# Weight pieces of half the columns, and a final norm whose last block is halved and whose one half ACT scales

## The chip, the cores and the metric

The kernel runs on one core of one Trainium2 chip. A core has five engines with instruction queues of their own: TensorE (PE, matmuls; its weight loads are listed apart as PEld), VectorE (DVE), ScalarE (ACT), GpSimd (POOL) and SyncE (SP, which here only starts DMAs). ACT's queue starts some DMAs too. Every queue runs in order. The metric is the device time of one execution, in microseconds (us); the time before is 828.61 us, the median of 3 runs (828.05 to 829.05).

## The reference, cut to what matters

Two layers over 512 tokens of width 1024, all in float32, each with a norm ahead and a residual behind, then a last norm:

```python
# layer 0
u = rms_norm(h, g0) @ w_in                    # 1024 -> 4096
v, gate = split(u)                            # 2048 each
p = multiscale_pool(v)                        # 4 groups of 512 columns, windows 2, 4, 8, 16
m = einsum('btgc,gcd->btgd', p, w_grp) * scale
h = h + (m * silu(gate)) @ w_out              # 2048 -> 1024
# layer 1
u = rms_norm(h, g1) @ w_in1                   # 1024 -> 8192
q, fz, i, gate = split(u)                     # 2048 each, 16 heads of 128
o = gated linear recurrence of q, fz, i       # per head, with a norm over the head
h = h + (o * silu(gate)) @ w_out1             # 2048 -> 1024
y = rms_norm(h, final_g)
```

## The kernel before, in words

**Matmuls.** Every large float32 product is made of three matmuls on rounded halves: a number is its rounded part (`hi`) plus the rest (`lo`), and hi x hi, hi x lo and lo x hi are added up in PSUM (`mm3`, L128 to L130). One such matmul has a 128x128 stationary operand and 512 columns of the moving one.

**Weights in pieces.** Weights come from DRAM in pieces of 128 partitions x 1024 numbers, 512 KB (`piece`, L99). SP starts the DMA into one of 3 raw buffers (`RAW`); ACT rounds it to `hi` (a cast, L96); DVE takes the difference for `lo` (L97). There are 6 buffers each for `hi` and `lo` (`WB`, L53). A buffer is free again when the last matmul that reads it is done. `load_in` cuts a block of 512 columns of an input matrix into pieces of two row tiles (two times 128 rows) and all 512 columns, so that 1024 rows make four pieces; `load_out` cuts 512 rows of an output matrix into four pieces of one row tile and all 1024 columns.

**Stages.** Work goes through four groups of 512 inner columns. In layer 0 a group is: values (L262), pooling on DVE, gates (L289), the group's 512x512 product (L303), and later the output product of the group before (`project_out`, L219). In layer 1 a group is: forget gates (L395) and queries (L411), inputs (the values of the recurrence, L422), the heads (L599 to L628), gates (L433), and the output product of the group before (`add_out`, L381). `project` (L146) makes one tile of 128 output columns: for each of the 8 row tiles its three matmuls, so one tile of an input stage is 24 matmuls and reads all four pieces, and a stage is four tiles. `inputs` is the other way round: the activations are stationary and the weights' 512 columns are streamed, so that it too reads all four pieces for each of its four token blocks.

**Order.** The program is written for a planner that orders each engine's queue by priority and by when operands should be ready, and adds the waits. The loads of weights have a raised priority (`AHEAD`, L57, `AHEAD0`, L56, and L104). A queue's order is fixed when the kernel is built; a waiting instruction holds up all behind it on its engine.

**The end.** `finish` (L503) loads the last four output pieces and the final weight vector (`fg`), and goes through the four token blocks. For each it makes two halves of 512 columns (`out_half`, L373: 12 matmuls, then a DVE add from PSUM into `ht`), each squared and summed on ACT (L514); then two one-column operations on DVE (L516, L517), the power -1/2 on POOL (L519), and the product with that factor and with `fg` on DVE, a half at a time (L523). ACT's queue stores the first half and SP's the second (L524). Behind that stands a conditional part that isn't run here (L763): every engine's queue reads a flag and branches past it, and then all engines meet.

Of the kernel before, what the change touches and what calls it, by code (L numbers as in the profile page):

```python
# [32 lines left out]
F32 = mybir.dt.float32  # L33
# [3 lines left out]
AF = mybir.ActivationFunctionType  # L37
ALU = mybir.AluOpType
PSUM = bass.MemoryType.PSUM

P = 128
D = 1024
T = 512
DI = 2048
# [5 lines left out]
TB = T // P  # L50
EPS = 1e-6
WINDOWS = (2, 4, 8, 16)
RAW, WB = 3, 6  # L53
WARM = 10
NORM_AT, SPREAD_AT = (KD - 2, 2), (KD - 1, 1)
AHEAD0 = 85  # L56
# [10 lines left out]
def trunk(ctx: ExitStack, tc: tile.TileContext, xT, x_d, par, ident_d, causal_d, mask_d, fg_d, w0_in, w0_grp, w0_out, w1_in, w1_out, out):  # L67
# [31 lines left out]
    def piece(src, ahead=AHEAD):  # L99

        raw = wpool.tile([P, 2, GC], F32, name="wraw", tag="wraw", bufs=RAW)
        hi = wpool.tile([P, 2, GC], F32R, name="whi", tag="whi", bufs=WB)
        lo = wpool.tile([P, 2, GC], F32R, name="wlo", tag="wlo", bufs=WB)
        with tc.high_priority(ahead):  # L104
            nc.sync.dma_start(out=raw, in_=src)
            split(raw, hi, lo)
        return hi, lo

    def load_in(w, col=0, ahead=AHEAD):
# [5 lines left out]
            out += [(hi[:, 0], lo[:, 0]), (hi[:, 1], lo[:, 1])]  # L115
        return out

    def load_out(w, g):

        out = []  # L120
        for i in range(GT):
            r = g * GC + i * P
            hi, lo = piece(w[r:r + P, :].rearrange("p (a b) -> p a b", a=2))
            out.append((hi.rearrange("p a b -> p (a b)"), lo.rearrange("p a b -> p (a b)")))
        return out

    def mm3(out, lh, ll, rh, rl, start, stop):
# [18 lines left out]
    def project(pieces, n, xs, at=None):  # L146


        if at:
            acc = pa.tile([P, T], F32, name="a", tag="a", bufs=4)  # L150
        else:
            acc = ps.tile([P, T], F32, name="mm", tag="mm", bufs=4)
        c = slice(n * P, (n + 1) * P)
        for k, ((wh, wl), (xh, xl)) in enumerate(zip(pieces, xs)):
            if at and k in at:
                at[k]()
            mm3(acc, wh[:, c], wl[:, c], xh, xl, k == 0, k == len(pieces) - 1)
        return acc

    def rms(name, srcs, cols=slice(0, T)):  # L160
# [57 lines left out]

    def project_out(pieces, zs):  # L219
        for n in range(KD):  # L220
            acc = project(pieces, n, zs)
            nc.vector.tensor_tensor(out=h[n], in0=acc, in1=h[n], op=ALU.add)  # L222


    with tc.tile_pool(name="l0", bufs=1) as l0:
# [18 lines left out]
            nc.sync.dma_start(out=xt, in_=x_d[b * P:(b + 1) * P, :])  # L244
            nc.scalar.activation(out=xt, in_=xt, func=AF.Square, accum_out=ss[:, b:b + 1])
        accs = project4(pieces, xs, None)
        wg0 = load_in(w0_in, DI, AHEAD0)
        norm = []

        def factor():  # L250
# [10 lines left out]

        def values(g):  # L262
            vs = []
            wv = None if g == 0 else load_in(w0_in, g * GC)
            for n in range(GT):
                acc = accs[n] if g == 0 else project(wv, n, xs)
                v = l0.tile([P, 16 + T], F32, name="v", tag="v", bufs=4)
                nc.gpsimd.memset(v[:, 0:16], 0.0)
                nc.vector.tensor_tensor(out=v[:, 16:], in0=acc, in1=rb, op=ALU.mult)
                vs.append(v)  # L270
            return vs
# [15 lines left out]
            return out  # L287

        def gates0(g):  # L289
            wg = wg0 if g == 0 else load_in(w0_in, DI + g * GC)  # L290
            out = []
            for n in range(GT):
                acc = gates[n] if g == 0 and n < 2 else project(wg, n, xs)
                gt = l0.tile([P, T], F32, name="gt", tag="gt", bufs=2)
                nc.vector.tensor_tensor(out=gt, in0=acc, in1=rb, op=ALU.mult)
                sg = l0.tile([P, T], F32, name="sg", tag="sg", bufs=2)
                nc.scalar.activation(out=sg, in_=gt, func=AF.Sigmoid)  # L297
                gs = l0.tile([P, T], F32, name="gs", tag="gs", bufs=4)
                nc.gpsimd.tensor_tensor(out=gs, in0=gt, in1=sg, op=ALU.mult)  # L299
                out.append(gs)  # L300
            return out

        def mixed(g, ps_, gates):  # L303
            wm = load_in(w0_grp[g])
            out = []
            for n in range(GT):
                acc = project(wm, n, ps_)
                z = small.tile([P, T], F32, name="z", tag="hg", bufs=2)
                c = C_PS + g * GT + n
                nc.vector.scalar_tensor_tensor(out=z, in0=acc, scalar=pp[:, c:c + 1], in1=gates[n], op0=ALU.mult, op1=ALU.mult)  # L310
                out.append(halves(z, "z", 8, l0))
            return out
# [36 lines left out]
    def hgrn(ctx, general):  # L349
# [20 lines left out]
                        nc.tensor.transpose(out=tp[:, i * P:(i + 1) * P], in_=h[half * (KD // 2) + i][:, b * P:(b + 1) * P], identity=ident)  # L370
                    nc.scalar.copy(out=ht[b][:, half * 512:(half + 1) * 512], in_=tp)

        def out_half(pieces, zs, b, half):  # L373

            acc = ps.tile([P, 512], F32, name="mm", tag="mm", bufs=4)
            t, c = slice(b * P, (b + 1) * P), slice(half * 512, (half + 1) * 512)
            for k, ((wh, wl), (zh, zl)) in enumerate(zip(pieces, zs)):
                mm3(acc, zh[:, t], zl[:, t], wh[:, c], wl[:, c], k == 0, k == len(pieces) - 1)
            nc.vector.tensor_tensor(out=ht[b][:, c], in0=acc, in1=ht[b][:, c], op=ALU.add)  # L379

        def add_out(pieces, zs):  # L381
            for b in range(TB):
                for half in range(2):
                    out_half(pieces, zs, b, half)

        def sigmoids(acc):
# [6 lines left out]
            return s1, s2  # L393

        def forget(g, store):  # L395
            wf = None if g == 0 else load_in(w1_in, DI + g * GC)
            fs, ks = [], []
            for pr in range(2):
                f = l1.tile([P, 2, T], F32, name="f", tag="f", bufs=2)
                kk = l1.tile([P, 2, T], F32, name="kk", tag="kk", bufs=2)  # L400
                for j in range(2):
                    n = 2 * pr + j
                    hd = g * GT + n
                    s1, s2 = sigmoids(accs[n] if g == 0 else project(wf, n, xs))
                    store(f, pr, j, hd, s1)
                    nc.vector.tensor_scalar(out=kk[:, j], in0=s2, scalar1=rest[:, hd:hd + 1], scalar2=None, op0=ALU.mult)
                fs.append(f)
                ks.append(kk)
            return fs, ks

        def queries(g):  # L411
            wq = load_in(w1_in, g * GC)
            qs = []
            for pr in range(2):
                q = l1.tile([P, 2, T], F32, name="q", tag="q", bufs=2)
                for j in range(2):
                    acc = project(wq, 2 * pr + j, xs)
                    nc.vector.tensor_tensor(out=q[:, j], in0=acc, in1=rb, op=ALU.mult)
                qs.append(q)
            return qs  # L420
# [56 lines left out]
        def group(g, prepare, heads, zs):  # L477
# [4 lines left out]
            if first:  # L482
                turn()
            if first or last:
                wg = load_in(w1_in, 3 * DI + g * GC)
                gts = gates1(wg, (0, 1))
                ons = [attend(n) for n in range(GT)]
                gts += gates1(wg, (2, 3))
            else:
                add_out(load_out(w1_out, g - 1), zs)  # L490
                ons = [attend(n) for n in range(GT)]
                gts = gates1(load_in(w1_in, 3 * DI + g * GC), range(GT))
            if first:
                l1.tile([P, 32], F32, name="pad2")
            now = [gated(g, n, ons[n], gts[n], last) for n in range(2)]
# [7 lines left out]
        def finish(zs):  # L503

            wo = load_out(w1_out, NG - 1)
            fg = [act.tile([P, 512], F32, name="fg", tag=f"xh{i}", bufs=1) for i in range(2)]
            for i in range(2):
                nc.scalar.dma_start(out=fg[i], in_=fg_d[:, i * 512:(i + 1) * 512])
            for b in range(TB):
                ss = l1.tile([P, 2], F32, name="ss", tag="ss", bufs=2)  # L510
                for half in range(2):
                    out_half(wo, zs, b, half)
                    sq = small.tile([P, 512], F32, name="sq", tag="sq", bufs=2)
                    nc.scalar.activation(out=sq, in_=ht[b][:, half * 512:(half + 1) * 512], func=AF.Square, accum_out=ss[:, half:half + 1])  # L514
                ms = small.tile([P, 1], F32, name="ms", tag="ms", bufs=4)
                nc.vector.tensor_tensor(out=ms, in0=ss[:, 0:1], in1=ss[:, 1:2], op=ALU.add)  # L516
                nc.vector.tensor_scalar(out=ms, in0=ms, scalar1=1.0 / D, scalar2=EPS, op0=ALU.mult, op1=ALU.add)  # L517
                rn = small.tile([P, 1], F32, name="rnf", tag="rnf", bufs=2)
                nc.gpsimd.tensor_tensor(out=rn, in0=ms, in1=mhalf[:, 0:1], op=ALU.pow)  # L519
                for half in range(2):  # L520
                    c = slice(half * 512, (half + 1) * 512)
                    y = act.tile([P, 512], F32, name="y", tag=f"x{'hl'[half]}{2 + b}", bufs=1)
                    nc.vector.scalar_tensor_tensor(out=y, in0=ht[b][:, c], scalar=rn, in1=fg[half], op0=ALU.mult, op1=ALU.mult)  # L523
                    (nc.sync if half else nc.scalar).dma_start(out=out[b * P:(b + 1) * P, c], in_=y)  # L524

        def factored():

# [285 lines left out]
```

## Time and profile before

| | |
|---|---|
| median of 3 runs | 828.61 us (828.05 to 829.05) |
| profiled execution, its own time | 828.94 us |
| its span (first to last instruction) | 827.1 us |
| PE busy | 816.1 us (99%), 3902 matmuls |
| PE's weight loads busy | 685.8 us (83%) |
| DVE busy | 546.2 us (66%) |
| ACT busy | 278.7 us (34%) |
| POOL busy | 150.3 us (18%) |
| granted TensorE clock, mean | 0.997 of full speed |
| DMA | 81.14 MB, mean 98 GB/s |

The profile was taken in one execution on the chip. The span is what the trace shows; the device time of the same execution holds 1.84 us more around it. Busy times of the engines lie beside each other, so they don't add up; what counts is which engine's work, or which wait, ends last. Matmuls overlap: one is listed as 0.39 us long while the next starts 0.227 us after it. The chain that ended last is PE 95%, DVE 3% and the rest below 1% each.

### The profile page before, as it was taken

How to read it: one execution, taken by the hardware profiler on the slowest of the kernel's cores; microseconds unless marked ns; L12 is line 12 of the kernel's file. 1: busy time of each engine (PE TensorE's matmuls, PEld its weight loads, DVE VectorE, ACT ScalarE, POOL GpSimd, SP SyncE). 2: the span in 40 equal slices, each digit the busy share in tenths (PEclk: the TensorE clock that was granted, in tenths of full speed). 3: DMA queues.
4: the chain of work that ended last, by engine and by line, in shares of the span. 5: the costliest groups of instructions: out<-in, count | busy, mean ns of one | idle time of the engine just before them, and what ended most of it. 6: DMA issues, size and time to landing. Idle time of an engine off the chain costs nothing.

```text
span 827.1 us, 10198 instructions
## 1 busy us (share of the span) xinstructions
PE 816.1 (99%) x3902; PEld 685.8 (83%) x3902; DVE 546.2 (66%) x837; ACT 278.7 (34%) x476; POOL 150.3 (18%) x197
## 2 busy tenths in 40 slices
PE   9999999999999999999999999999999999999995
PEld 8888888888888888888888888888888888888884
DVE  5687537854785465798169973359973459973744
ACT  7442134223234244325342241343240333242311
POOL 0030010002011032260313400313300313302100
PEclk9999999999999999999999999999999999999998
DMA  9531324223232155133033240333240333240302
GB/s 342 198 103 52 101 102 153 78 71 116 94 101 103 55 178 178 52 102 102 1 102 102 77 128 1 103 102 102 77 128 1 103 101 102 77 126 3 102 14 92
DMA packets 37769, 81.14 MB, mean 98 GB/s; under 512 B 2896, under 2 KB 3152, under 8 KB 37712
## 3 DMA queue, kind: packets, MB, share of 16 engines
q1 hardware_dynamic: 35264, 76.56, 28.3%
q10 hardware_dynamic: 2448, 3.86, 1.3%
q8 instruction: 32, 0.52, 0.3%
q14 instruction: 25, 0.20, 0.1%
HBM read 76.21 MB, written 4.19 MB: 97 GB/s over the span
## 4 chain that ended last, share of the span: by engine, by line
PE 95%; DVE 3%; issue 1%; DMA 0%; ACT 0%; POOLq 0%; POOL 0%; DVEq 0%; ACTq 0%
PE mm L128 29%; PE mm L129 28%; PE mm L130 28%; PE a L625 2%; PE a L627 1%; PE a L588 1%; PE a L605 1%; DVE r L572 1%; PE a L466 1%; DVE wlo L97 1%; PE a L83 1%; PE a L594 0%; DMA wraw<-in_w1i 0%; PE a L128 0%; PE a L130 0%
## 5 line engine op out<-in xcount | busy, mean ns | idle before, releaser
L128 PE MATMUL mm<-xh,whi 128*128 128x512 f32 x624 | 244.7, 392 | 0.0
L129 PE MATMUL mm<-xl,whi 128*128 128x512 f32 x624 | 243.2, 390 | 0.0
L130 PE MATMUL mm<-xh,wlo 128*128 128x512 f32 x624 | 243.0, 390 | 0.0
L96 ACT CAST whi<-wraw 128x1024 fp32r<-128x1024 f32 (+1 forms) x140 | 141.8, 1026 | 237.3 <-PE mm L129 108.6
L97 DVE TENSOR_TENSOR wlo<-wraw,whi 128x1024 fp32r<-128x1024 f32 (+1 forms) x140 | 172.0, 1253 | 56.6 <-ACT whi L96 54.5
L130 PEld LDWEIGHTS mm<-xh,wlo 128*128 128x128 f32 x624 | 117.3, 188 | 24.6
L128 PEld LDWEIGHTS mm<-xh,whi 128*128 128x128 f32 x624 | 117.4, 188 | 24.1 <-DVE h L222 0.3
L129 PEld LDWEIGHTS mm<-xl,whi 128*128 128x128 f32 x624 | 117.3, 188 | 24.2
L572 DVE RECIPROCAL r<-r 128x512 f32<-128x512 f32 x16 | 53.4, 3338 | 0.0
L128 PE MATMUL mm<-whi,xh 128*128 128x512 f32 x128 | 50.1, 391 | 0.0
L129 PE MATMUL mm<-wlo,xh 128*128 128x512 f32 x128 | 50.0, 391 | 0.0
L130 PE MATMUL mm<-whi,xl 128*128 128x512 f32 x128 | 49.9, 390 | 0.0
L129 PE MATMUL mm<-zl,whi 128*128 128x512 f32 x128 | 49.8, 389 | 0.0
L128 PE MATMUL mm<-zh,whi 128*128 128x512 f32 x128 | 49.8, 389 | 0.0
L130 PE MATMUL mm<-zh,wlo 128*128 128x512 f32 x128 | 49.8, 389 | 0.0
L379 DVE TENSOR_TENSOR ht<-mm,ht 128x512 f32<-128x512 f32 x32 | 22.0, 688 | 35.1 <-PE mm L130 35.1
L222 DVE TENSOR_TENSOR h<-mm,h 128x512 f32<-128x512 f32 x32 | 21.9, 688 | 28.4 <-PE mm L130 28.1
L442 POOL TENSOR_TENSOR gs<-fz,s 128x512 f32<-128x512 f32 x16 | 21.5, 1342 | 98.7 <-ACT s L440 98.7
L299 POOL TENSOR_TENSOR gs<-gt,sg 128x512 f32<-128x512 f32 x16 | 21.9, 1372 | 87.8 <-ACT sg L297 87.8
L128 PE MATMUL mm<-whi,z1h 128*128 128x512 f32 x96 | 37.6, 392 | 0.0
L130 PE MATMUL mm<-whi,z1l 128*128 128x512 f32 x96 | 37.4, 390 | 0.0
L129 PE MATMUL mm<-wlo,z1h 128*128 128x512 f32 x96 | 37.4, 389 | 0.0
(151 smaller groups left out, 1156.0 us busy)
## 6 DMA issues: line engine op xcount, KB each, us to landing
wraw<-in_w1i SPq DMA_DIRECT2D x64, 512.0 KB, 3.9
wraw<-in_w0i SPq DMA_DIRECT2D x28, 512.0 KB, 4.3
wraw<-in_w0o SPq DMA_DIRECT2D x16, 512.0 KB, 3.7
wraw<-in_w1o SPq DMA_DIRECT2D x16, 512.0 KB, 4.3
wraw<-in_w0g SPq DMA_DIRECT2D x8, 512.0 KB, 3.9
h<-in_xT SPq DMA_DIRECT2D x8, 256.0 KB, 5.1
wraw<-in_w0i SPq DMA_DIRECT2D x8, 256.0 KB, 5.3
xt<-in_x SPq DMA_DIRECT2D x4, 512.0 KB, 6.7
```

The source lines that it names most:

```text
L83: nc.tensor.matmul(warm[:, :P], ones, ones, start=True, stop=True)
L96: nc.scalar.copy(out=hi, in_=src)
L97: nc.vector.tensor_tensor(out=lo, in0=src, in1=hi, op=ALU.subtract)
L128: nc.tensor.matmul(out, lh, rh, start=start, stop=False)
L129: nc.tensor.matmul(out, lh, rl, start=False, stop=False)
L130: nc.tensor.matmul(out, ll, rh, start=False, stop=stop)
L222: nc.vector.tensor_tensor(out=h[n], in0=acc, in1=h[n], op=ALU.add)
L299: nc.gpsimd.tensor_tensor(out=gs, in0=gt, in1=sg, op=ALU.mult)
L379: nc.vector.tensor_tensor(out=ht[b][:, c], in0=acc, in1=ht[b][:, c], op=ALU.add)
L442: nc.gpsimd.tensor_tensor(out=gs, in0=gt, in1=sg, op=ALU.mult)
L572: nc.vector.reciprocal(out=r, in_=r)
L625: nc.tensor.matmul(o[:, b], Ads[pr][:, j, t], v[:, b, n * P:(n + 1) * P], start=True, stop=b == 0)
```

## The change

It does five things.

1. Input weights are cut by `load_cols` instead of `load_in` wherever `project` uses them: pieces of four row tiles and 256 columns, so that the first two tiles of a stage read two pieces and the last two tiles the other two. `load_in` stays for layer 0's first block, for `inputs`, and for layer 1's first block.
2. Output weights (`load_out`) are cut into pieces of two row tiles and 512 columns; `project_out` and `add_out` go through the left 512 columns with two pieces and then the right 512 with the other two. For `add_out` this turns the loops: half outside, token block inside.
3. `WB` goes from 6 to 5.
4. In `finish` all four blocks' left halves are made first. POOL multiplies each by `fg` while the rest goes on. The right halves follow; the last one is made as two groups of 256 columns.
5. The square carries the factor 1/sqrt(1024), so that the sum needs only EPS added. After the power, DVE multiplies the right half by factor and `fg`, and ACT multiplies the left half, prepared by POOL, by the factor in place.

```diff
-RAW, WB = 3, 6
+RAW, WB = 3, 5
 ...
+    def load_cols(w, col=0, ahead=AHEAD):
+        v = w.rearrange("(k p) n -> p k n", p=P)
+        out = []
+        for i in range(2):
+            cut = []
+            for k in range(0, v.shape[1], 4):
+                c = col + i * 256
+                hi, lo = (x.rearrange("p a (b c) -> p (a b) c", b=2) for x in piece(v[:, k:k + 4, c:c + 256], ahead))
+                cut += [(hi[:, j], lo[:, j]) for j in range(4)]
+            out += [[(hi[:, j * P:(j + 1) * P], lo[:, j * P:(j + 1) * P]) for hi, lo in cut] for j in range(2)]
+        return out
 ...
     def load_out(w, g):
+        v = w[g * GC:(g + 1) * GC, :].rearrange("(k p) n -> p k n", p=P)
         out = []
-        for i in range(GT):
-            r = g * GC + i * P
-            hi, lo = piece(w[r:r + P, :].rearrange("p (a b) -> p a b", a=2))
-            out.append((hi.rearrange("p a b -> p (a b)"), lo.rearrange("p a b -> p (a b)")))
+        for c in range(0, D, GC):
+            got = [piece(v[:, k:k + 2, c:c + GC]) for k in range(0, GT, 2)]
+            out.append([(hi[:, j], lo[:, j]) for hi, lo in got for j in range(2)])
         return out
 ...
         def add_out(pieces, zs):
-            for b in range(TB):
-                for half in range(2):
+            for half in range(2):
+                for b in range(TB):
                     out_half(pieces, zs, b, half)
 ...
+            ss = l1.tile([P, TB, 3], F32, name="ss")
+            first = [act.tile([P, 512], F32, name="y", tag=f"xh{2 + b}", bufs=1) for b in range(TB)]
+            def square(b, c0, n, i):
+                sq = small.tile([P, 512], F32, name="sq", tag="sq", bufs=2)
+                nc.scalar.activation(out=sq[:, :n], in_=ht[b][:, c0:c0 + n], func=AF.Square, scale=D ** -0.5, accum_out=ss[:, b, i:i + 1])
+            for half in range(2):
+                for b in range(TB):
+                    if half == 0:
+                        out_half(wo, zs, b, half)
+                        square(b, 0, 512, 0)
+                        nc.gpsimd.tensor_tensor(out=first[b], in0=ht[b][:, :512], in1=fg[0], op=ALU.mult)
+                        continue
+                    ms = small.tile([P, 1], F32, name="ms", tag="ms", bufs=4)
+                    if b < TB - 1:
+                        out_half(wo, zs, b, half)
+                        square(b, 512, 512, 1)
+                        nc.vector.tensor_scalar(out=ms, in0=ss[:, b, 0:1], scalar1=EPS, scalar2=ss[:, b, 1:2], op0=ALU.add, op1=ALU.add)
+                    else:
+                        for i in range(2):
+                            out_half(wo, zs, b, half, i * 256, 256)
+                            square(b, 512 + i * 256, 256, 1 + i)
+                            if i == 0:
+                                nc.vector.tensor_scalar(out=ss[:, b, 0:1], in0=ss[:, b, 0:1], scalar1=EPS, scalar2=ss[:, b, 1:2], op0=ALU.add, op1=ALU.add)
+                        nc.vector.tensor_tensor(out=ms, in0=ss[:, b, 0:1], in1=ss[:, b, 2:3], op=ALU.add)
+                    rn = small.tile([P, 1], F32, name="rnf", tag="rnf", bufs=2)
+                    nc.gpsimd.tensor_tensor(out=rn, in0=ms, in1=mhalf[:, 0:1], op=ALU.pow)
+                    y = act.tile([P, 512], F32, name="y", tag=f"xl{2 + b}", bufs=1)
+                    nc.vector.scalar_tensor_tensor(out=y, in0=ht[b][:, 512:], scalar=rn, in1=fg[1], op0=ALU.mult, op1=ALU.mult)
+                    nc.sync.dma_start(out=out[b * P:(b + 1) * P, 512:], in_=y)
+                    nc.scalar.activation(out=first[b], in_=first[b], func=AF.Copy, scale=rn)
+                    nc.scalar.dma_start(out=out[b * P:(b + 1) * P, :512], in_=first[b])
```

## Rows read from the trace of the kernel before

**Rows 1.** The page: engine's busy us (share), instructions; granted clock in 40 slices, tenths.
```profile
PE 816.1 (99%) x3902; PEld 685.8 (83%) x3902; DVE 546.2 (66%) x837; ACT 278.7 (34%) x476; POOL 150.3 (18%) x197
...
PEclk9999999999999999999999999999999999999998
```
**Rows 2.** Waits of PE, whole span: waiter, waited for, us, times, longest.
```profile
PE a L594 <- ACT kt L596: 0.3, 1, 0.3
PE a L605 <- DVE Ad L591: 0.2, 1, 0.2
```
**Rows 3.** Timeline, end of PE: start, us, engine, line, operation [idle before].
```profile
817.08 0.39 PE L129 MATMUL mm<-wlo,zz 128*128 128x512 f32 x1
817.08 0.19 PEld L130 LDWEIGHTS mm<-whi,zz 128*128 128x128 f32 x1
817.31 0.39 PE L130 MATMUL mm<-whi,zz 128*128 128x512 f32 x1
```
**Rows 4.** Groups by line and shape, PEld: count | busy us, mean ns | idle before.
```profile
L588 PEld LDWEIGHTS a<-q,kk 128*128 128x128 f32 x128 | 15.8, 192 | 0.3
```
**Rows 5.** Timeline, all engines, from PE's last matmul.
```profile
817.73 0.69 DVE L379 TENSOR_TENSOR ht<-mm,ht 128x512 f32<-128x512 f32 x1 [0.82 <-PE mm L130]
818.52 0.63 ACT L514 ACTIVATE sq<-ht 128x512 f32<-128x512 f32 x1 [0.79 <-DVE ht L379]
...
819.27 0.16 DVE L516 TENSOR_TENSOR ms<-ss 128x1 f32<-128x1 f32 x1 [0.85 <-ACT sq L514]
819.47 0.15 DVE L517 TENSOR_SCALAR ms<-ms 128x1 f32<-128x1 f32 x1
...
820.34 1.41 DVE L523 SCALAR_TENSOR_TENSOR y<-ht,rnf,fg 128x512 f32<-128x512 f32 x2 [0.72 <-POOL rnf L519]
821.12 0.34 ACTq L524 DMA_DIRECT2D out_y<-y  x1
821.78 0.33 SPq L524 DMA_DIRECT2D out_y<-y  x1
```
**Rows 6.** Lines 763, 809 (program's end): queue, count: min/median/max ns, first to last start.
```profile
L763 SPq EVENT_SEMAPHORE  x8: 17/17/17, 825.2 to 825.7; - x8
...
L763 ACTq EVENT_SEMAPHORE  x1: 17/17/17, 825.3 to 825.3; - x1
...
L809 POOLq EVENT_SEMAPHORE  x4: 17/17/17, 826.3 to 827.0; - x4
```
**Rows 7.** Groups by line and shape, DVE, ACT, POOL (columns as rows 4).
```profile
L591 DVE COPY_PREDICATED Ad<-causal,a 128x256 f32<-128x256 uint8 x16 | 6.9, 429 | 0.0
...
L450 ACT ACTIVATE oq<-a 128x128 f32<-128x128 f32 x64 | 16.7, 285 | 5.3 <-PE a L627 3.6 <-POOL gs L442 1.5
...
L209 ACT ACTIVATE xh<-h,pp 128x512 fp32r<-128x512 f32 x16 | 11.6, 726 | 8.7 <-DVE h L222 6.4 <-DMA pp<-in_par 1.6 <-DMA h<-in_xT 0.6
...
L442 POOL TENSOR_TENSOR gs<-fz,s 128x512 f32<-128x512 f32 x16 | 21.5, 1342 | 98.7 <-ACT s L440 98.7
```
**Rows 8.** DMA issues: queue, count, KB each, median us from issue to landing.
```profile
wraw<-in_w0o SPq DMA_DIRECT2D x16, 512.0 KB, 3.7
wraw<-in_w0g SPq DMA_DIRECT2D x8, 512.0 KB, 3.9
...
fg<-in_fg ACTq DMA_DIRECT2D x2, 256.0 KB, 3.1
```
**Rows 9.** Chain that ended last, 378 to 389: start, us, what.
```profile
378.90 3.78 DMA wraw<-in_w1i
```
**Rows 10.** Timeline, heads of layer 1's second group (columns as rows 3).
```profile
491.55 0.43 DVE L591 COPY_PREDICATED Ad<-causal,a 128x256 f32<-128x256 uint8 x1
...
491.66 2.51 PE L605 MATMUL a<-vn,kt 128*128 128x128 f32 x21
```
**Rows 11.** Timeline, from queries to inputs of the second group (columns as rows 3).
```profile
466.21 3.97 DVE L97 TENSOR_TENSOR wlo<-wraw,whi 128x1024 fp32r<-128x1024 f32 x3
...
469.31 0.40 PE L129 MATMUL mm<-wlo,xh 128*128 128x512 f32 x1
```

More of the change, by code (lines that the diff above doesn't have):

```diff
@@ L104, in piece @@
         with tc.high_priority(ahead):
-            nc.sync.dma_start(out=raw, in_=src)
+            nc.sync.dma_start(out=raw if src.shape[1] == 2 else raw.rearrange("p a (b c) -> p (a b) c", b=2), in_=src)
             split(raw, hi, lo)
@@ L152, in project @@
             acc = ps.tile([P, T], F32, name="mm", tag="mm", bufs=4)
-        c = slice(n * P, (n + 1) * P)
-        for k, ((wh, wl), (xh, xl)) in enumerate(zip(pieces, xs)):
+        for k, ((wh, wl), (xh, xl)) in enumerate(zip(pieces[n], xs)):
             if at and k in at:
                 at[k]()
-            mm3(acc, wh[:, c], wl[:, c], xh, xl, k == 0, k == len(pieces) - 1)
+            mm3(acc, wh, wl, xh, xl, k == 0, k == len(xs) - 1)
         return acc
@@ L220, in project_out @@
         for n in range(KD):
-            acc = project(pieces, n, zs)
+            acc = project([[(hi[:, c:c + P], lo[:, c:c + P]) for hi, lo in half] for half in pieces for c in range(0, GC, P)], n, zs)
             nc.vector.tensor_tensor(out=h[n], in0=acc, in1=h[n], op=ALU.add)
@@ L246, in trunk @@
         accs = project4(pieces, xs, None)
-        wg0 = load_in(w0_in, DI, AHEAD0)
+        wg0 = load_cols(w0_in, DI, AHEAD0)
         norm = []
@@ L263, in values @@
             vs = []
-            wv = None if g == 0 else load_in(w0_in, g * GC)
+            wv = None if g == 0 else load_cols(w0_in, g * GC)
             for n in range(GT):
@@ L289, in gates0 @@
         def gates0(g):
-            wg = wg0 if g == 0 else load_in(w0_in, DI + g * GC)
+            wg = wg0 if g == 0 else load_cols(w0_in, DI + g * GC)
             out = []
@@ L303, in mixed @@
         def mixed(g, ps_, gates):
-            wm = load_in(w0_grp[g])
+            wm = load_cols(w0_grp[g])
             out = []
@@ L371, in turn, with out_half @@
                     nc.scalar.copy(out=ht[b][:, half * 512:(half + 1) * 512], in_=tp)
[L373 to L378, printed above, removed]
+        def out_half(pieces, zs, b, half, c0=0, n=512):
+            acc = ps.tile([P, 512], F32, name="mm", tag="mm", bufs=4)[:, :n]
+            t, c, d = slice(b * P, (b + 1) * P), slice(half * 512 + c0, half * 512 + c0 + n), slice(c0, c0 + n)
+            for k, ((wh, wl), (zh, zl)) in enumerate(zip(pieces[half], zs)):
+                mm3(acc, zh[:, t], zl[:, t], wh[:, d], wl[:, d], k == 0, k == GT - 1)
             nc.vector.tensor_tensor(out=ht[b][:, c], in0=acc, in1=ht[b][:, c], op=ALU.add)
         def add_out(pieces, zs):
-            for b in range(TB):
-                for half in range(2):
+            for half in range(2):
+                for b in range(TB):
                     out_half(pieces, zs, b, half)
@@ L395, in forget @@
         def forget(g, store):
-            wf = None if g == 0 else load_in(w1_in, DI + g * GC)
+            wf = None if g == 0 else load_cols(w1_in, DI + g * GC)
             fs, ks = [], []
@@ L411, in queries @@
         def queries(g):
-            wq = load_in(w1_in, g * GC)
+            wq = load_cols(w1_in, g * GC)
             qs = []
@@ L484, in group @@
             if first or last:
-                wg = load_in(w1_in, 3 * DI + g * GC)
+                wg = load_cols(w1_in, 3 * DI + g * GC)
                 gts = gates1(wg, (0, 1))
@@ L491, in group @@
                 ons = [attend(n) for n in range(GT)]
-                gts = gates1(load_in(w1_in, 3 * DI + g * GC), range(GT))
+                gts = gates1(load_cols(w1_in, 3 * DI + g * GC), range(GT))
             if first:
@@ L508, in finish @@
                 nc.scalar.dma_start(out=fg[i], in_=fg_d[:, i * 512:(i + 1) * 512])
[L509 to L524, printed above, removed]
```

## The prediction

> **What bounds the kernel now.** I read the busy table and the clock row first: TensorE (PE) is busy 816.1 of 827.1 us, at the 2.4 GHz level in all but the last slice [rows 1]. Then who PE waited for: after the start only 0.3 us for an ACT copy and 0.2 us for a DVE copy [rows 2], both in the first group of layer 1. So between its first and last matmul the program is PE's own work, and no faster load or split can take more than that 0.5 to 0.6 us out of it. What is left is the end: the last matmul starts at 817.31 [rows 3] and the span ends at 827.1. The timeline of those 9.8 us [rows 5] is one chain: add of the last 128x512 block (817.73), square (818.52), two one-column operations (819.27, 819.47), the power on POOL, two products on DVE from 820.34, the store from SP at 821.78; after it the end of the program [rows 6]. The change can win in that chain, and can lose wherever PE comes to wait.
>
> **Part 1, the final norm, counted on that chain.**
> Add: 256 columns instead of 512. No DVE add from PSUM of 256 columns is shown; the nearest row, a 256-column copy from PSUM, takes 0.43 [rows 7] against 0.69 [rows 5]. I take 0.42: -0.27 (bounds: half of 0.69 and all of it, -0.35 to 0).
> Square: 0.63 at 512 columns [rows 5], 0.285 at 128 [rows 7]; the line through both gives 0.40 at 256: -0.23 (bounds -0.32 to 0).
> Small operations: one instead of two, 819.47 - 819.27 = -0.20.
> Products: DVE makes only one after the power, so SP's store need not wait for the second: -0.70 (half of 1.41).
> Together -1.40.
> Matmuls: 12 of 512 columns at 0.227 (817.31 - 817.08) [rows 3], 2.72 us, become 24 of 256. 512 columns at 2.4 GHz are 0.213, so 0.0135 of the spacing doesn't shrink; 0.1067 + 0.0135 = 0.120, and 24 x 0.120 = 2.88: +0.16. Lower bound 0 (pure halving). Upper bound: if a weight load, 0.19 long [rows 3], could not overlap the next load, the spacing would be 0.188 and the price 24 x (0.188 - 0.113) = +1.8. Against that, 128 loads of the 128-column products, 0.192 each, kept their unit busy only 15.8 us, 0.123 apiece [rows 4]: loads do overlap, so I stay at +0.16.
> The Trainium skill (TensorE: Matmul & The Clock Gate, "Measured speedup vs the span model") says that a weight load runs beside a matmul only when it goes to other row groups; to the letter, load and stream would add up in each of the 24 matmuls, and the whole sum below would be a loss. The trace disagrees: the load listed at 817.08 starts together with a matmul and is over before the next one [rows 3].
> DVE order: with half-major order the block before the last has its own norm 2.7 us before the end, not 5.4. Its last matmul starts at 817.31 - 12 x 0.227 = 814.59, its add 0.42 later (as 817.73 follows 817.31), at 815.01, and its product 2.61 - 0.20 after that (817.73 to 820.34, less one small operation), at 817.42, until 818.12. That product stands before the last add, which is ready at 817.73 + 0.16 = 817.89; behind it comes the small sum for the first half piece (0.15). So the last add starts near 818.25: +0.35. Bounds: 0 (product placed behind the add), and +1.4 if DVE keeps the written order: product to 818.12, then the first half's add to 818.45, its square on ACT, the small sum at 819.2, and only then the last add, at 819.3.
> ACT's side: the first half is no product on DVE but a scaled copy, 0.73 [rows 7], that ends with DVE's. ACT's store then goes at about 820.6 + 0.35 = 820.95 instead of 821.12 [rows 5], only 0.15 to 0.2 earlier. In the program's end ACT reports at 825.3, SP from 825.2 to 825.7, and all meet at 826.3 [rows 6]: ACT has 1.0 in hand. SP's path moves 0.9 forward and ACT's 0.15, so 0.25 of that is left: no cost, at most +0.2.
> POOL's four new products with the weight vector, 1.34 each for 512 columns [rows 7], fall beside the first four blocks' matmuls, 10.9 us in which POOL has nothing else; without that cover one of them would hold up a power by up to 1.34, but a block's power comes four blocks after its product. The scale inside the square and EPS as an immediate ride in operations that are there anyway.
> Sum of part 1: -1.40 + 0.16 + 0.35 = -0.89, from -1.40 to +0.4 (written order: -1.40 + 0.16 + 1.43 is +0.2, with ACT's 0.2), the load bound of +1.8 kept for a rival.
>
> **Part 2, the pieces.** Each is still 512 KB, four to a stage, so DMA issues, casts (ACT) and differences (DVE) stay as many and as long; SP's queue only waits for free buffers. What moves is when PE needs a piece and gives it back. A stage of four tiles is 96 matmuls, 21.8 us. Before, the first tile touched all four pieces, and all came back in the last 4.1 us; of the next stage's pieces the third and fourth, which go into the first two buffers given back, had 4.1 + 2.7 = 6.8 us from release to use. With half the columns the first pair is back 8.2 and 10.9 us into the stage. With five buffers the next stage's second piece takes the first of these, 13.6 us before the stage ends, and is used 2.7 into its own: 16 us, against 2.3 for cast and difference; the fourth, whose buffer comes back 2.7 before the end, is used at 13.6: 16 as well. The same holds for the output weights, whose halves are worked one after the other, 10.9 us each. Only the value projection of layer 1 still holds four pieces to its end. Into it, the fourth piece keeps the old 6.8 us and the second and third get more. Out of it, the order of casts is the old one, one piece earlier. I count 0 for all this.
> The rows in DRAM are shorter: 1 KB in the input weights (2 KB before), 2 KB in the output weights (4 KB before). 512 KB land in 3.9 us with 2 KB rows and 3.7 with 4 KB rows [rows 8], so halving once more is +0.2. No 1 KB row is shown at this size. Bounds: 0; and, if the moving part went by rows, its doubling: 256 KB land in 3.1, so half a piece is 0.8 of moving and a whole one 1.6: +1.6. I take +0.2, the nearest.
> The Trainium skill (DMA: Bandwidth & Descriptors, "Why small descriptors are slow (HBM only)") puts about 3 cycles on each packet, 32 bytes a cycle; by it two 1 KB rows take 70 cycles for the 67 of one 2 KB row, an estimate of +0.17 us on a piece. No run here shows it yet.
> Where does +0.2 meet PE? Nearly every load lies far ahead. The exception is the piece that is loaded as the value projection ends: in the first group the chain runs through its transfer, 3.78 long [rows 9], then its cast and difference, to the copies behind these on ACT and DVE that PE waits for in [rows 2]. There +0.2 counts in full. In the later groups the copy ends at 491.98 and PE needs it after the first state product, six of the instructions of which 21 take 2.51 from 491.66, near 492.35 [rows 10]: some 0.35 of slack hides it.
> Part 2: +0.2, from -0.55 (the wait goes because the order shifts) to +4 (below).
>
> **Sum.** -0.89 + 0.2 = -0.7 us. The profiled run was 828.94 (span 827.1 and 1.84 around it), which makes 828.2; the median of the three runs is 0.33 lower, so 827.9.
>
> **Rivals.**
> A, both go right: the product before the last falls clear of the last add and the wait in group one disappears: -1.40 + 0.16 = -1.24, less 0.55: -1.8, 826.8. For it: PE's wait hangs on one blocked DVE difference. Against it: the same piece is still cast at the same place.
> B, the norm's gain is eaten on DVE: the written order holds: -1.40 + 0.16 + 1.43 + 0.2 = +0.4, 829.0. For it: in the trace DVE does wait for the power with nothing else in between (0.72 before 820.34). Against: there nothing else was ready.
> C, weight loads set the pace at 256 columns: -1.40 + 1.8 + 0.35 + 0.2 = +0.95, 829.5; if load and stream even add up (0.19 + 0.107 each, +4.4 in all), 832.1. Against: [rows 4].
> D, 1 KB rows are slow (slower): +1.6 a piece hits group one in full, groups two and three less 0.35: -0.89 + 1.6 + 2 x 1.25 = +3.2, 831.8. It decides once a piece lands over 1.1 us later than now. Against: the 0.2 between 4 and 2 KB.
> E, five buffers (slower): at the change from queries to the value projection DVE runs three differences in a row from 466.21 to 470.18, and PE uses the second at 469.31 [rows 11], 0.46 after it ends. If with one buffer fewer the planner puts it third, PE waits 470.18 - 469.31 = 0.87 in each of three groups: -0.7 + 2.6 = +1.9, 830.5. Against: it should come first there, since the two before it are now split long before.
>
> **How the numbers follow.** Forecast 0.50, A 0.17, B 0.10, C 0.04, D 0.09, E 0.10. About 0.2% (1.66 us) is what can be told from no change: under 826.95 is faster, over 830.27 slower. Faster is A, 0.17; slower D and E, 0.19; the rest, 0.64, is within. The range 826.6 to 830.2 leaves out D and E alone.
>
> **What would show it.** In the profile after: the last add of 256 columns near 0.42, its start within 0.4 us of PE's last group; one DVE product after the last power; 256-column matmuls 0.12 apart; PE's waits still under 1 us in all; pieces landing in about 4.1 us; SP's last store about 0.9 us closer to PE's last matmul. I am wrong if PE shows waits of over 1 us for casts or differences, or if the stretch from the last matmul to the last store is not shorter.

## The result, and the profile after

The changed kernel takes 832.94 us (median of 5 runs, 832.69 to 833.11) against 828.15 for the kernel before (827.96 to 829.05): a ratio of 1.0055, 95% interval 1.0040 to 1.0069. It is 4.8 us slower, and outside the predicted range. The profiled run took 833.06 with a span of 831.3, against 828.94 and 827.1.

PE still does the same work: the page of the kernel after has its busy time 1.3 us up and its clock row unchanged [rows 1].
```profile
PE 817.4 (98%) x3914; PEld 686.5 (83%) x3914; DVE 542.4 (65%) x831; ACT 285.4 (34%) x482; POOL 162.4 (20%) x201
...
PEclk9999999999999999999999999999999999999998
```
What is new is waiting. First PE's waits behind DVE in the whole span of the kernel after, then DVE's that has no row of its kind before (waiter, waited for, us, times, longest). These answer to [rows 2].
```profile
PE mm L144 <- DVE wlo L97: 2.6, 3, 0.9
...
PE a L637 <- DVE Ad L623: 0.5, 2, 0.2
```
```profile
DVE r L604 <- POOL r L603: 13.9, 6, 3.3
```
The three waits of PE at L144 are one place in three groups, in the value projection (the stage `inputs`). Here is the first of them, in the timeline of PE, DVE and POOL of the kernel after (start, us, engine, line, operation, idle before and who ended it). It answers to [rows 11].
```profile
462.99 3.72 POOL L603 TENSOR_SCALAR r<-f 128x512 f32<-128x512 f32 x2 [0.46 <-DVE q L608]
...
465.29 3.35 DVE L604 RECIPROCAL r<-r 128x512 f32<-128x512 f32 x1 [1.38 <-POOL r L603]
468.56 2.83 DVE L97 TENSOR_TENSOR wlo<-wraw,whi 128x1024 fp32r<-128x1024 f32 x2
...
468.51 0.39 PE L143 MATMUL mm<-whi,xh 128*128 128x512 f32 x1
469.77 0.50 PE L144 MATMUL mm<-wlo,xh 128*128 128x512 f32 x1 [0.88 <-DVE wlo L97]
```
Read it backwards. PE has the high part (whi) of the value projection's last piece at 468.51 and its low part (wlo) only at 469.77. That difference is the first of the pair from 468.56, and it stands on DVE behind a reciprocal that began at 465.29, after DVE had waited for POOL's clamp. In the kernel before, the same piece was the second of a row that began at 466.21 [rows 11].

The other places were found by lining up PE's stages. A row gives the start of a stage in the kernel before, and how much later (us) the same matmul starts in the others: A the kernel after; the other four are runs told of below (five buffers with the old pieces, six buffers with the new, four raw buffers, the clamp on DVE).
```
stage, its start before          A     five old  six new  raw four  clamp on DVE
layer 1 begins         329.76  -0.36   -0.16    +0.40    -0.28    -0.72
value projection, gr 2 464.87  -0.57   -0.20    +0.26    -0.93    +0.63
heads, group 2         486.78  +0.60   +1.07    +0.24    +0.21    +0.61
after the heads, gr 2  494.26  +1.45   +1.06    +1.13    +0.24    +1.59
value projection, gr 3 589.45  +1.43   +1.07    +1.12    +0.24    +1.57
heads, group 3         611.55  +2.42   +2.16    +0.91    +1.24    +1.35
value projection, gr 4 714.23  +2.41   +2.15    +0.90    +1.26    +1.35
heads, group 4         736.17  +3.55   +3.39    +0.85    +2.39    +1.30
after the heads, gr 4  743.64  +3.93   +3.39    +0.86    +2.42    +1.30
final norm's matmuls   795.59  +3.92   +3.39    +0.85    +2.41    +1.30
end of the span        827.1   +4.2    +3.4     +1.1     +2.7     +1.5
```
Layer 0 is no slower in this profile. A shift of some tenths is there after 28 us and is no part of a change: three kernels whose body is that of the kernel before, below, start layer 1 at -0.40, -0.73 and -0.31. From 464.87 on, the kernel after loses 1.17, 0.99 and 1.14 in the value projections, 0.85 in the heads of the second group and 0.38 in those of the fourth: 4.5, of which 3.3 is one place three times. One profile each stands behind the table. A second profile of the same body (the pieces alone, below; the slowest of its five runs) repeats the value projections (1.14, 0.96, 1.13) and the fourth group's heads (0.37), but loses 1.52 in the second group's heads, and 1.1 in layer 0, so those two places change from execution to execution.

Then the end. The timeline of the kernel after, engine by engine: PE's last matmuls, DVE's last adds and products, ACT's last square and store. It answers to [rows 3, 5].
```profile
818.74 0.28 PE L143 MATMUL mm<-whi,zz 128*128 128x256 f32 x1
818.85 0.28 PE L144 MATMUL mm<-wlo,zz 128*128 128x256 f32 x1
818.97 0.28 PE L145 MATMUL mm<-whi,zz 128*128 128x256 f32 x1
...
821.49 0.28 PE L145 MATMUL mm<-whi,zz 128*128 128x256 f32 x1
...
816.58 0.68 DVE L393 TENSOR_TENSOR ht<-mm,ht 128x512 f32<-128x512 f32 x1
...
819.61 1.18 DVE L393 TENSOR_TENSOR ht<-mm,ht 128x512 f32<-128x512 f32 x2
...
821.95 0.75 DVE L553 SCALAR_TENSOR_TENSOR y<-ht,rnf,fg 128x512 f32<-128x512 f32 x1 [0.65 <-POOL rnf L551]
...
822.74 0.41 DVE L393 TENSOR_TENSOR ht<-mm,ht 128x256 f32<-128x256 f32 x1
823.73 0.16 DVE L549 TENSOR_TENSOR ms<-ss 128x1 f32<-128x1 f32 x1 [0.57 <-ACT sq L528]
824.55 0.75 DVE L553 SCALAR_TENSOR_TENSOR y<-ht,rnf,fg 128x512 f32<-128x512 f32 x1 [0.66 <-POOL rnf L551]
...
823.19 0.42 ACT L528 ACTIVATE sq<-ht 128x256 f32<-128x256 f32 x1 [0.52 <-DVE ht L393]
...
825.30 0.37 ACTq L556 DMA_DIRECT2D out_y<-y  x1
```
The last add could start at about 821.8 and starts at 822.74, behind the product of the block before; its square is followed by one small operation, one power, one product. Both queues send their last store at 825.3. From the first matmul of this stage (795.59 before, 799.51 after) the last store on SP is at 25.80, from 26.19; the one on ACT at 25.79, from 25.53 [rows 5]. The span ends 6.0 us after ACT's store in both kernels (827.1 - 821.12, 831.3 - 825.30), so the end seems to go with ACT's: the new ending costs 0.3 and brings nothing.

In the median the pieces land no later for their shorter rows (`in_w0i` x28 and `in_w0g` are all in 1 KB rows now, `in_w1i` in part): the page's DMA issues of the kernel after (queue, count, KB each, median us to landing), for [rows 8].
```profile
wraw<-in_w1i SPq DMA_DIRECT2D x64, 512.0 KB, 3.6
wraw<-in_w0i SPq DMA_DIRECT2D x28, 512.0 KB, 3.7
...
wraw<-in_w0g SPq DMA_DIRECT2D x8, 512.0 KB, 3.6
```

### The profile page after: what moved, and what is told of

Its sections match the earlier page's. It is cut to its first block, busy times and chain, and to the rows that moved or that the text cites. A ratio compares the mean times of both kernels' runs of the same rounds, so it can differ in the third digit from the quotient of the medians.

```text
span 831.3 us, 10236 instructions
## 1 busy us (share of the span) xinstructions
PE 817.4 (98%) x3914; PEld 686.5 (83%) x3914; DVE 542.4 (65%) x831; ACT 285.4 (34%) x482; POOL 162.4 (20%) x201
## 4 chain that ended last, share of the span: by engine, by line
PE 81%; DVE 10%; issue 3%; POOL 3%; DMA 2%; ACT 1%; POOLq 0%; DVEq 0%; ACTq 0%
PE mm L144 24%; PE mm L145 24%; PE mm L143 24%; DVE wlo L97 3%; DVE r L604 3%; PE a L657 2%; POOL r L603 1%; PE a L659 1%; PE a L637 1%; DMA wraw<-in_w1i 1%; DVE q L432 1%; DVE f L589 1%; DVE f L590 1%; ACT whi L96 1%; PE a L83 1%
## 5 line engine op out<-in xcount | busy, mean ns | idle before, releaser
L144 PE MATMUL mm<-xl,whi 128*128 128x512 f32 x624 | 243.1, 390 | 0.0
L97 DVE TENSOR_TENSOR wlo<-wraw,whi 128x1024 fp32r<-128x1024 f32 (+1 forms) x140 | 168.4, 1207 | 96.9 <-ACT whi L96 95.1
L96 ACT CAST whi<-wraw 128x1024 fp32r<-128x1024 f32 (+1 forms) x140 | 143.9, 1028 | 254.8 <-PE mm L144 180.1
L144 PEld LDWEIGHTS mm<-xl,whi 128*128 128x128 f32 x624 | 117.3, 188 | 24.1
L604 DVE RECIPROCAL r<-r 128x512 f32<-128x512 f32 x16 | 53.5, 3345 | 13.9 <-POOL r L603 13.9
L144 PE MATMUL mm<-wlo,xh 128*128 128x512 f32 x128 | 50.2, 392 | 2.6 <-DVE wlo L97 2.6
L144 PE MATMUL mm<-zl,whi 128*128 128x512 f32 x128 | 49.8, 389 | 0.0
L456 POOL TENSOR_TENSOR gs<-fz,s 128x512 f32<-128x512 f32 x16 | 26.4, 1650 | 97.8 <-ACT s L454 97.8
L313 POOL TENSOR_TENSOR gs<-gt,sg 128x512 f32<-128x512 f32 x16 | 24.4, 1526 | 89.6 <-ACT sg L311 89.6
L393 DVE TENSOR_TENSOR ht<-mm,ht 128x512 f32<-128x512 f32 (+1 forms) x33 | 22.2, 672 | 28.6 <-PE mm L145 28.5
L144 PE MATMUL mm<-wlo,z1h 128*128 128x512 f32 x96 | 37.4, 389 | 0.0
L468 POOL TENSOR_TENSOR ro<-mo,mhalf 128x4 f32<-128x4 f32 x16 | 16.2, 1016 | 100.6 <-DVE mo L466 100.6
```

Of the source, the lines that this page charges most:

```text
L96: nc.scalar.copy(out=hi, in_=src)
L97: nc.vector.tensor_tensor(out=lo, in0=src, in1=hi, op=ALU.subtract)
L144: nc.tensor.matmul(out, lh, rl, start=False, stop=False)
L468: nc.gpsimd.tensor_tensor(out=ro[:, :, 0], in0=mo, in1=mhalf[:, :TB], op=ALU.pow)
L604: nc.vector.reciprocal(out=r, in_=r)
```

## The experiments

**Which half costs.** The change was taken apart: the pieces with the old final norm (`pieces_only`), and the new final norm with the old pieces (`norm_only`).
```diff
 pieces_only = the kernel after, but
-        def finish(zs):   # in the new form
+        def finish(zs):   # as before
 norm_only = the kernel before, but
-        def finish(zs):   # as before
+        def finish(zs):   # in the new form, out_half with columns c0 to c0 + n
```


> The changed kernel with the final norm of before: all of the change's pieces, five buffers, half-major output products, and the old ending. Theory (the loss is in layer 1's body, where PE starts the last stretch 3.9 us late, and the new ending is worth about nothing): 3.7 to 4.2 us slower than before, PE waits of 0.88 each for the weight differences at the three changes from queries to inputs. Rival (the new ending gives the 0.9 that was forecast, the body costs more): over 4.8 us slower.

> The kernel before with the new final norm alone (half-major, last block halved, POOL and ACT for the left half), old pieces, six buffers. Theory (DVE's products come before the next block's add and push it, and ACT's store now ends last): 0 to 0.5 us slower than before. Rival (forecast): 0.9 us faster. PE's only waits stay those of the kernel before, 0.5 us.

Measured: the pieces alone 832.68 (832.11 to 834.46), ratio 1.0051 [1.0037, 1.0064]; the norm alone 828.60 (828.44 to 829.43), ratio 1.0003 [0.9994, 1.0012]. Within these intervals the whole loss is the pieces'; the norm gives nothing, where -0.9 was forecast. In the norm-only profile the last stores are at 820.77 (ACT) and 820.79 (SP), 25.79 and 25.81 after the stage's first matmul at 794.98: as in the kernel after.

**The sixth buffer, under the new pieces.**
```diff
-RAW, WB = 3, 5
+RAW, WB = 3, 6
```


> The changed kernel with six buffers for the halves instead of five, nothing else. Theory (what counts is the order of DVE's queue, which comes from the pieces of half the columns; it is the same row for row in layer 1's second to fourth group with six buffers): within 0.3 us of the changed kernel, PE waits of 0.88 at the same three places. Rival (the fifth buffer is missing): the waits go, 2.6 to 3.9 us faster than the changed kernel.

Measured 830.02 (829.64 to 830.63), ratio 1.0019 [1.0010, 1.0028]. My reading at that time, that the order on DVE alone makes the waits, fell: the order stayed row for row, DVE still waits 13.9 us for POOL, and yet the three waits of 0.88 are gone:
```profile
PE mm L144 <- DVE pl L97: 0.8, 1, 0.8
...
DVE r L604 <- POOL r L603: 13.9, 6, 3.2
...
466.12 3.35 DVE L604 RECIPROCAL r<-r 128x512 f32<-128x512 f32 x1 [1.38 <-POOL r L603]
469.38 2.84 DVE L97 TENSOR_TENSOR wlo<-wraw,whi 128x1024 fp32r<-128x1024 f32 x2
```
The pair behind the late reciprocal is still there, but it no longer holds a piece that PE needs at once: with one buffer more each cast is one piece ahead. That is 2.9 of the loss. The other 1.5 (830.02 against 828.51, the kernel before in the same set of runs) stays with six buffers: the table has 0.89 of it in the second group's heads, and in this profile the wait of 0.8 above, for the low part of a pooled tile at 53 us, puts layer 0 1.1 later (from -0.56 to +0.55); the profile of the pieces alone has such a wait too, the kernel after has none there, and why is open.

**POOL's clamp.** DVE waits at that place because the clamp in front of the reciprocals runs on POOL. Here DVE does it.
```diff
-                        nc.gpsimd.tensor_scalar(out=r, in0=fs[pr][:, j], scalar1=FLOOR, scalar2=None, op0=ALU.max)
+                        nc.vector.tensor_scalar(out=r, in0=fs[pr][:, j], scalar1=FLOOR, scalar2=None, op0=ALU.max)
```


> The changed kernel with the clamp ahead of each reciprocal on DVE instead of POOL (16 operations). Theory (DVE idles 4.6 us a group for POOL's clamp, with no weight difference left to fill the gap, and so makes the last difference for inputs late): DVE's idle time before reciprocals goes from 13.9 us to near 0, the three PE waits of 0.88 vanish, 2.5 to 4 us faster than the changed kernel although DVE gets some 8 us of work. Rival (the waits come from loads or from the casts on ACT): PE's waits stay.

Measured 830.75 (830.41 to 831.82), ratio 1.0030 [1.0018, 1.0042]: 2.2 below the kernel after, somewhat under the 2.5 to 4 that were expected. With five buffers still, the three waits are gone, since the reciprocal starts without the hop to POOL and the pair comes earlier:
```profile
462.36 0.42 DVE L603 TENSOR_SCALAR r<-f 128x512 f32<-128x512 f32 x1
...
463.03 3.35 DVE L604 RECIPROCAL r<-r 128x512 f32<-128x512 f32 x1
466.29 2.83 DVE L97 TENSOR_TENSOR wlo<-wraw,whi 128x1024 fp32r<-128x1024 f32 x2
```
Part is given back in the heads of the first group, where PE now waits 1.0 for a DVE copy. So the wait needs both: a piece that is cast late, and a DVE that gets to it late. Either cure removes it.

**The fifth buffer, under the old pieces.**
```diff
 the kernel before
-RAW, WB = 3, 6
+RAW, WB = 3, 5
```


> The kernel before with five buffers in place of six and nothing else; DVE's queue keeps its order through layer 1. Theory one (a missing buffer sends the difference of the last input piece one place later, whatever the pieces' shape): it becomes the last of the three that start at 466.21 us in the kernel before, ends near 470.2 and PE wants it at 469.3, so PE waits 0.9 in each of three groups, 2.6 us in all: about 831. Theory two (the loss needs both: fewer buffers, and the new pieces, whose casts sit where DVE stands still for POOL's clamp): no PE wait on a difference and 828.2 to 828.8.

Measured 832.29 (832.19 to 832.86), ratio 1.0049 [1.0035, 1.0062], 1.3 above the 831 of theory one. This settles the larger part: one buffer fewer, the pieces whole, and 4.0 of the loss is there. Its DVE rows, for [rows 11], and PE:
```profile
462.76 3.34 DVE L572 RECIPROCAL r<-r 128x512 f32<-128x512 f32 x1
466.02 3.96 DVE L97 TENSOR_TENSOR wlo<-wraw,whi 128x1024 fp32r<-128x1024 f32 x3
...
466.14 0.39 PE L128 MATMUL mm<-whi,xh 128*128 128x512 f32 x1
467.23 0.50 PE L129 MATMUL mm<-wlo,xh 128*128 128x512 f32 x1 [0.70 <-DVE wlo L97]
...
468.50 0.39 PE L128 MATMUL mm<-whi,xh 128*128 128x512 f32 x1
468.90 0.50 PE L129 MATMUL mm<-wlo,xh 128*128 128x512 f32 x1
```
The row of three on DVE has kept its time (466.02 for 466.21, with the whole kernel 0.20 early), but each place in it holds the piece before: second, third and fourth of the projection instead of third, fourth and one of the next stage. So PE waits at the head of the row, 0.86 more than the usual 0.23 between these two matmuls, and 0.17 at the next; with the slower restarts 1.27 in this group, then 1.09 and 1.24 (the table). Theory one put 0.9 on each at the last piece; the wait came at the second, with the mechanism that it named. Theory two is out.

**The raw buffers.** The loss of 0.85 in the second group's heads is absent with the old pieces. In the kernel after it has a chain of its own (the chain of waits):
```profile
483.54 1.06 ACT whi L96
484.62 1.24 DVE wlo L97
485.88 4.69 DMA wraw<-in_w1i
490.65 1.05 ACT whi L96
491.73 1.23 DVE wlo L97
...
493.30 0.34 DVE Ad L623
```
```diff
 the kernel after
-RAW, WB = 3, 5
+RAW, WB = 4, 5
```


> The changed kernel with four buffers for raw pieces in place of three. It asks where the 0.83 us in the heads of the second group come from: there the chain of waits goes through a transfer of a raw piece (4.7 us) that starts only when a difference frees its buffer. Theory one (the raw buffer sets it): the transfer starts one piece earlier, the matmuls on Ad don't wait, and the time falls by 0.6 to 1.0, to about 832; the three waits of 0.88 on the differences stay, since they hang on the split pieces' buffers. Theory two (the buffers of the split pieces set it there too): the same as the changed kernel within 0.3, 832.7 to 833.1.

Measured 831.05 (830.84 to 831.55), ratio 1.0033 [1.0021, 1.0044], 1.9 below the kernel after; the expected 0.6 to 1.0 was for this place alone. So the expectation was missed by 0.9. The fourth cast of that row no longer waits for its transfer, so its difference is early and the copies of Ad (the masked products of the heads) are in time:
```profile
488.44 1.21 DVE L97 TENSOR_TENSOR wlo<-wraw,whi 128x1024 fp32r<-128x1024 f32 x1
...
492.11 0.43 DVE L623 COPY_PREDICATED Ad<-causal,a 128x256 f32<-128x256 uint8 x1
```
The table shows the second group's heads at no loss (+0.21 to +0.24) and the fourth's next to none (0.03, from 0.38); another 0.4 comes from the first group, after which this kernel stands at -0.93 and the kernel after at -0.57; the three waits in the value projections stay, as theory one says. Six buffers together with four raw ones were not tried.

**The end, with the order on DVE set by hand.** The planner puts the product of a block ahead of the next block's add. Here it is held behind it, on the kernel before with the new norm (`norm_held_dve`); then ACT's scaling is held behind the next square as well, and one of ACT's stores goes to SP (`norm_held_both`).
```diff
+                            with tc.issue_after(add.ins):            # norm_held_both: and after the square
+                                held.pop()()                         # product, store, scaling of the block before
...
-                    nc.vector.scalar_tensor_tensor(out=y, in0=ht[b][:, 512:], scalar=rn, in1=fg[1], op0=ALU.mult, op1=ALU.mult)
+                    held.append(product)                             # the same four calls, as a function
```


> The kernel before with the new final norm, in which DVE's product of a block is put behind the next block's last addition (the order that the written program does not have). Theory one (DVE's late products are all that delays the end): the last addition starts 0.85 to 0.93 earlier, and the time falls by 0.7 to 0.9 against the new norm alone, to 827.7 to 827.9. Theory two (ACT's scaling of the block before, 0.72 plus a store's issue of 0.37, stands ahead of the last square in the same way): the square moves by only 0.1, and the time stays within 0.3 of the new norm alone, 828.2 to 828.8.

> As the run before, and ACT's scaling of a block is put behind the next block's last square too; the store of the scaled half of the last block but one goes to SP's queue, so that ACT's next scaling isn't behind its issue. If both engines' products of the block before are what delays the end, the last products start 0.75 earlier than in the new norm alone and both last stores too: 827.5 to 827.9, and 0.4 to 0.9 under the kernel before. If the ending is set by what follows the last store whatever its start, the same as the new norm alone: 828.3 to 828.8.

Measured: DVE alone 828.19 (827.73 to 828.58), ratio 0.9998 [0.9989, 1.0007]; both 828.34 (827.71 to 828.92), ratio 0.9999 [0.9990, 1.0008]. Neither can be told from the kernel before by its time. 828.19 lies 0.01 under the range of theory two, and 828.34 in the range of the second case, the same as the new norm alone. The profiles say more. With DVE alone:
```profile
817.17 0.43 DVE L379 TENSOR_TENSOR ht<-mm,ht 128x256 f32<-128x256 f32 x1 [0.22 <-PE mm L130]
...
817.69 0.34 ACTq L551 DMA_DIRECT2D out_y<-y  x1
818.07 0.42 ACT L515 ACTIVATE sq<-ht 128x256 f32<-128x256 f32 x1 [0.41 <-ACT y L550]
...
820.18 0.37 ACTq L551 DMA_DIRECT2D out_y<-y  x1
```
The last add now waits for PE alone, 0.31 after the last matmul (816.86), 0.94 earlier in the stage than in the kernel after, and then its square waits for ACT's scaling and store of the block before and is only 0.49 earlier. With both held:
```profile
817.95 0.42 ACT L515 ACTIVATE sq<-ht 128x256 f32<-128x256 f32 x1 [0.86 <-DVE ht L379]
...
819.30 0.75 DVE L548 SCALAR_TENSOR_TENSOR y<-ht,rnf,fg 128x512 f32<-128x512 f32 x1 [0.66 <-POOL rnf L544]
...
820.05 0.37 ACTq L551 DMA_DIRECT2D out_y<-y  x1
```
Counted from the stage's first matmul, ACT's last store stands at 25.53 before, 25.79 in the new norm, 25.30 with DVE held (820.18 - 794.88), 24.85 with both (820.05 - 795.20); the span ends at 31.47, 31.72, 31.21 and 31.04. In these profiles, one of each kernel, the order was the obstacle, on two engines one after the other, and 0.4 is what the new end then gives. That is less than the interval of the times, and the medians don't show it (0.06 above the kernel before with both held, 0.09 with the new norm alone), so a version that beats the kernel before was not shown.

## Why the prediction was wrong

The step that failed is Part 2's "I count 0 for all this", for five buffers. It followed each piece from the release of its buffer to its use and found 16 us of slack, or the old 6.8 at the value projection, and took a slack of that size for cover. But those 6.8 us (7.75 in the trace: the transposes between the two stages were left out) were full. In the kernel before, the last piece is cast at 461.33 and used at 469.08. From 458.25 on DVE has two reciprocals with products between them, and the piece's difference is second in the row behind these, from 466.21 [rows 11]:
```profile
458.25 3.34 DVE L572 RECIPROCAL r<-r 128x512 f32<-128x512 f32 x1
...
461.33 1.06 ACT L96 CAST whi<-wraw 128x1024 fp32r<-128x1024 f32 x1 [0.30 <-PE mm L129]
...
462.95 3.34 DVE L572 RECIPROCAL r<-r 128x512 f32<-128x512 f32 x1
```
In the kernel after it is products, the wait for POOL's clamp and one reciprocal, until 468.56. The order of casts did stay "the old one, one piece earlier" in one sense: each place in DVE's row had the piece before. I took that as harmless and it is the loss. A sixth buffer was worth one piece of lead at the value projection, as the runs with five and six show; without it PE waits in each of three groups, 3.3 us with the new pieces, 3.6 with the old.

Rival E had the missing buffer, the place and the three groups, at 0.10. Its condition, the piece one place later in DVE's row, holds with five buffers and the old pieces; in the kernel after the piece is late by another way, so that its 0.87 a group comes near the listed wait of 0.88 is in part luck. The groups lost 1.0 to 1.2: the wait is counted from the end of a matmul that is listed as 0.39 long, while the low part comes 1.03 later than the usual 0.23 (468.51 to 469.77), and the restart costs about 0.1 more. It lacked the two other terms, the heads and the end. What spoke against it, "it should come first there, since the two before it are now split long before", is how the pair does stand in the kernel after (the needed piece is its first); the pair itself was 2.35 later (468.56 for 466.21), because DVE met POOL's clamp, and what stood next in its queue was the reciprocal that needs it.

The other steps:
- 256-column matmuls 0.120 apart, forecast +0.16: measured 0.12 (818.74, 818.85, 818.97). Right, and rival C is out. The Trainium skill (TensorE: Matmul & The Clock Gate, "The mechanism", where the sentence that the prediction uses stands) has a weight load overlap a matmul only when it goes to other row groups, so that load and stream would add up here; the rows disagree, with loads of 0.19 on record [rows 3] and matmuls 0.12 apart.
- Add 0.42, square 0.40, one small operation, one product on DVE: 0.41, 0.42, one, one. The -1.40 is there: from the last add to SP's last store it is 4.05 before (817.73 to 821.78) and 2.59 after (822.74 to 825.33).
- DVE order +0.35: mis-sized, 0.93 (822.74 against 821.8). I reckoned one block, and for one block it was right. The delay carries over from block to block: each late add makes its own product late, which is in the way of the next add. Counted in steps of 2.72 from an add that waits for PE alone (813.49), the next two adds, at 816.58 and 819.61, are late by 0.37 and 0.68.
- ACT's side, "ACT has 1.0 in hand", at most +0.2: wrong. The span ends 5.9 to 6.2 after ACT's last store in all ten profiles, and 5.2 to 6.2 after SP's (5.3 in the kernel before); so SP's store seems to have had 0.66 to give before it counted (that is read from the distances alone, and no run tests it). That, and the 0.93, turn -0.89 into +0.3.
- 1 KB rows +0.2 on a landing: not seen, and rival D's +1.6 refuted, by the medians, 3.6 for 3.9 (`in_w0g`) [rows 8]. The 0.2 between 4 and 2 KB rows was no firm step either: on the page before, 4 KB rows land in 3.7 and 4.3 (`in_w0o`, `in_w1o`). The packets' own records do show a price: in the kernel after, a 1 KB packet takes 46 ns in the median and a 2 KB one 84, so two short ones take 8 more. If a piece is spread evenly over the 16 DMA engines, that is 16 pairs on each and 0.13 us a piece, an estimate. That is near the estimate of +0.17 from the Trainium skill (DMA: Bandwidth & Descriptors, "Why small descriptors are slow (HBM only)"); the landings don't show it. Single transfers of 4.69 and 4.21 stand on the chain; why they are longer than the median stays open.
- "Where does +0.2 meet PE?" named the piece that is loaded as the value projection ends. In the first group, where it was to count in full, nothing was lost (-0.36 to -0.57). In the second that place did lose, 0.85, where I had seen 0.35 of slack [rows 10]; with a fourth raw buffer, and the same rows in DRAM, the loss is gone.

What stays open: why the planner's row of differences fell behind the clamp with the new pieces (it may be the releases that come earlier), why layer 0 loses 1.1 in two of the five profiles with the new pieces, and the 0.1 to 0.3 by which the losses of the value projections differ from group to group.

## What to carry to other kernels

Before a buffer is taken from a ring, list on the engine that fills it what stands between release and use: a slack that is long in time but full of queued work is no slack, and one place fewer shows as one wait per round. An end that is shortened on one queue is worth at most the lead that the other has on it, and here nothing; find the last event that the end follows at a fixed distance before counting a gain. A delay in a written or planned order repeats per block, so follow it over the blocks.

## What the runs showed of the hardware

A small POOL copy lasted until DVE's operations with two operands in SBUF beside it were done. The copy of 128x8 took 1.46 us in the kernel after, at 439.97, and ended at 441.43, just behind a DVE difference that ran from 440.16 to 441.38. It took 0.33 at 460.50, where one of DVE's products ended at 460.77, and 4.35 at 350.34, beside thirteen such products that ended at 354.63. Beside a reciprocal it took 0.19 (360.96).
```profile
439.97 1.46 POOL L594 COPY ends<-f 128x8 f32<-128x8 f32 x1 [16.93 <-DVE f L589]
440.16 1.22 DVE L97 TENSOR_TENSOR wlo<-wraw,whi 128x1024 fp32r<-128x1024 f32 x1
...
460.36 0.41 DVE L590 TENSOR_TENSOR f<-f 128x256 f32<-128x256 f32 x1
460.50 0.33 POOL L594 COPY ends<-f 128x8 f32<-128x8 f32 x1 [6.76 <-DVE f L589]
```
The clamps on POOL behind it are what DVE then waits for, 3.25 us in front of the reciprocal at 444.63.
